# One list schedule for everything up to the branch, and the second phase's buffers laid by the first phase's grounds

## The chip, the core and the metric

The kernel runs on one core of one Trainium2 chip. The metric is the device time of one execution in microseconds (us), lower being better.

## What is computed

One layer of a hybrid decoder over 4096 tokens of width 1024, batch 1, one layer deep:

```python
h = rmsnorm(x, g_pre) * (1 + scale) + shift          # shift, scale, gate = silu(c) @ ada_w + ada_b
proj = h @ w_in                                      # 1024 -> 3328, split by heads
attn = sliding_window_attention(aq, ak, av, sinks) * silu(ag)   # window 128, ALiBi
rkv  = rkv + (shift1(rkv) - rkv) * mu_rkv
rwkv = rwkv7(h, rr, rk, rv, ...) * silu(rg)          # delta rule, a state of 64x64 per head
gla  = gla(h, gq, gkk, gv, ...) * silu(gg)           # gated linear attention in chunks
y = concat([attn, rwkv, gla]) @ w_out
return x + gate * rmsnorm(y, g_post)
```

## The kernel before

The tokens are cut into NS = 16 tiles of NT = 256. Products with the large weights are made of float16 parts: each weight and each activation is split into a high and a low half, and three products of halves are added.

Phase 1 goes over the 16 tiles and does the normalisation, the recurrent groups (RWKV-7 and GLA) and all preparation. Its stages are generators: `stage_a` (norm and transposes of tile i, hT), `stage_p` (projections; it has the values "vg" ready first, then x1, then the k, r and v rows), `stage_d` (decays), `stage_qa`, `stage_qb`, `stage_qc` (matrix AT, its transfer through DRAM as adr into AS, a serial inverse TT in 15 steps on VectorE, its transfer as tdr into td, the assembled inverse tf), `stage_v`, `stage_k` (BK from KB), `stage_r` (GLA), and `stage_q2` (the recurrence over four chunks: rp, up, sp, and the state Sst from Ss and cd; then the normalised output ysb, sent to DRAM as mscr). Beside them run three streams of preparation:

- `stage_l` splits the later phase-1 weights.
- `stage_c(i)` splits the seven weights of phase 2 (w2): for each, eight pieces are loaded (cs) and squared, the sum goes through a matmul, and the pieces are loaded again, split (ch) and stored (wscr). After that it takes the squares of the output weight (`wo_squares`, twice 16 pieces) and forms and splits its combinations (`wo_group`, 16 of them, stored as woscr). `stage_c(i)` waits for `stage_c(i-1)` and for tile i's "vg".
- `stage_g` forms the adaLN gate from ada_w on GpSimd: two halves (gacc) of four blocks, each of two loads (gaw) with products and sums, then one pair of matmuls (gp) and a store.

`emit()` runs the generators by rank (a lower rank first) against an estimated TensorE clock and so writes the program; the place in it is each step's rank. While it is written, `Order.note` records each instruction with its estimated cost and what it must follow: readers and writers of the same data, the turn of a tile in its ring of buffers, the PSUM banks. `Order.pin()` then makes a list schedule of all recorded steps: engine by engine, the step that can start first and, among those, the one of lowest rank. It pins that order with dependencies which cost no semaphore. The rank of evictions in phase 2 is lowered by URGENT = 150.

Phase 1's buffers lie in five pools, work1a to work1d (the tuple `order` says which tag goes into which of the first three, the rest go into d) and c1p. After phase 1 these pools close, and phase 2 opens its own on the same ground: work2k (q, kT, vt, v4), c2p (ab), wg (weights q5 and q6), work2m (mxa, mxb), work2p (pr), work2o (yv, sm1), wb (output weights). The framework adds the waits that this reuse needs.

Then comes what is written ahead of a branch: the load of the weights (`stage_w`), the first projections (`stage_first`: `qkv(0)` with kp, two qp and vp; `gates(0)` with four gp, on q3 to q6; `qkv(1)`), tile 0's attention (`stage_s(0)`: scores sc into pr, exponentials, transposes, products ovp), and the loads of the output weights. The branch itself (line 1967) takes a slow path when a gate is out of limits, which it isn't with these inputs. In the kernel before, `pin()` is called at the end of phase 1, inside its block, and `forget()` throws away what was recorded from there to the branch: those instructions have no list schedule and are ordered by the framework alone. Behind the branch phase 2's main loop is recorded and pinned by a second `pin()`.

All instructions are issued through `Lane`, so the profile gives line 330 for nearly all of them, and names of tiles tell them apart. DMAs go through SP's one queue, in order.

Of the kernel before, what the change touches and what calls it, by code (L numbers as in the profile page):

```python
# [25 lines left out]
NS = T // NT  # L26
# [20 lines left out]
class Pool:  # L47


    def __init__(self, pool, bufs, held):  # L50
        self.pool, self.bufs, self.held = pool, bufs, held

    def tile(self, shape, dt, bufs=None, **kw):
        t = self.pool.tile(shape, dt, **kw) if bufs is None else self.pool.tile(shape, dt, bufs=bufs, **kw)
        self.held[t.tensor.name] = self.bufs if bufs is None else bufs
        return t


# [6 lines left out]
class Order:  # L65
# [2 lines left out]

    def __init__(self, tc):
        self.tc, self.held, self.masks, self.lag, self.urgent, self.joint = tc, {}, {}, 0, 0, 0  # L70
        self.steps = []
        self.wrote, self.read, self.users, self.slots, self.known = {}, {}, {}, {}, set()

    def pool(self, pool, bufs=1):
        return Pool(pool, bufs, self.held)

    def region(self, ap):

# [20 lines left out]
    def note(self, eng, name, outs, ins, func, r):  # L99
# [7 lines left out]
        n = max(math.prod(a.shape[1:]) for a in [o, *ins[:1]])  # L107
# [60 lines left out]
        for t, tensor in tiles.items():  # L168
            if t not in self.known:
                self.known.add(t)  # L170
                if t in self.held and tensor.tag:
                    held = self.slots.setdefault((tensor.owner_uid, tensor.tag), [])

                    if held and self.users.get(held[-1]):
                        st.turn.append(self.users[held[-1]][0])
                    if len(held) == self.held[t]:
                        for j in self.users.get(held.pop(0), ()):
                            need(j)
                    held.append(t)
            elif t in self.held and self.users.get(t):  # L180
                st.turn.append(self.users[t][0])
            if str(tensor.space) == "PSUM":
                for j in self.users.get(t, ()):
                    need(j)
# [209 lines left out]
def hybrid_kernel(ctx, tc, x, vecs, rows, adaw, w1, wl, w2, wo, w2aug, a2, gk2, cst, ctr, ctg, abias, out):  # L394
    nc = tc.nc
    model = Model(tc)
# [6 lines left out]
    def pool_of(at, name, bufs=1, **kw):  # L403
        return model.order.pool(at.enter_context(tc.tile_pool(name=name, bufs=bufs, **kw)), bufs)
# [141 lines left out]
    def streams(*lst):  # L546
        for rank, name, gen, i in lst:
            live.append([rank, i if i is not None else 0, name, gen(i), (), 0.0, ()])
# [92 lines left out]
    with ExitStack() as p1:  # L641
# [2 lines left out]
        pp = pool_of(p1, "c1p", 1)  # L644
        order = (("hf", "gl", "b1", "zs", "gw", "cgc", "bl", "gk1s", "zl0", "zl1", "zl2", "ch", "cl", "cs"),
                 ("zb0", "zb1", "zb2", "ta", "ep", "em", "b2", "KB"),
                 ("qg", "kg", "egp", "egm", "vg", "c2", "kt", "cd", "em0"))

        def wt(shape, name, bufs=1, dt=F32, tag=None):
            tag = tag or name  # L650
# [283 lines left out]
        def stage_c(i):  # L934

            yield [("c", i - 1), ("vg", i)]
            if 6 <= i < 8:
                yield from wo_squares(i - 6)
            elif 8 <= i < NS - 2:
                for g in range(i - 8, 16, 6):  # L940
                    yield from wo_group(g % 4, g // 4)
            for n in range(7):
                if n != i:
                    continue
                src = w2[:, n * 2048 : (n + 1) * 2048]
                inv = w_inv[n]


                def piece(j):
                    s32 = wt([P, 256], "cs", 2)  # L950
                    SP.dma_start(s32, src[:, j * 256 : (j + 1) * 256])
                    return s32

                ss = st.tile([P, 2, KD], F32, tag="wss8", name="wss8")
                for j in range(KD):
                    s32 = piece(j)
                    yield [s32]
                    S.activation(wt([P, 2, 256], "ch", 2, F16)[:, 0], s32, AF.Square, accum_out=ss[:, 0, j : j + 1])
                    if n == 2:
                        S.activation(wt([P, 2, 256], "ch", 2, F16)[:, 0][:, 0:P], s32[:, 0:P], AF.Square, accum_out=ss[:, 1, j : j + 1])  # L960
                yield [ss]
                parts = ((0, inv, None),) if n != 2 else ((0, inv, None), (1, k_sc[:, 1:2], k_sc[:, 0:1]))
                sc = st.tile([P, 1], F32, tag="wsc", name="wsc")
                for o, iv, sx in parts:
                    sst = st.tile([P, 1], F32, tag="wss", name="wss")
                    V.tensor_reduce(sst, ss[:, o, :], axis=AX.X, op=ALU.add)
                    yield [sst, "mq"]
                    sp = mq("wssp")
                    PE.matmul(sp[:, 0:1], ones, sst, start=True, stop=True)
                    tot = st.tile([P, 1], F32, tag="wtot", name="wtot")  # L970
                    V.tensor_copy(tot, sp[:, 0:1])
                    pow2(sc if sx is None else sx, iv, tot)
                for j in range(KD):
                    s32 = piece(j)
                    yield [s32]
                    hi, lo = [t[:, n] for t in (wt([P, 2, 256], "ch", 2, F16),) for n in range(2)]
                    S.activation(hi, s32, AF.Identity, scale=sc)
                    V.scalar_tensor_tensor(lo, s32, sc, hi, op0=ALU.mult, op1=ALU.subtract)
                    SP.dma_start(wscr[n, :, 0, j * 256 : (j + 1) * 256], hi)
                    SP.dma_start(wscr[n, :, 1, j * 256 : (j + 1) * 256], lo)  # L980
                if n == 2:

                    V.tensor_scalar(kq_s, inv, k_sc[:, 0:1], 2.0**-13, op0=ALU.mult, op1=ALU.mult)
                    V.tensor_mul(fneg[:, 0:1], hinv, k_sc[:, 1:2])
                    for m in range(2):
                        f2 = lsc.rearrange("p (v j) -> p v j", v=2)[:, :, 2 * m : 2 * m + 2]
                        V.tensor_scalar(fneg[:, 1:2], fneg[:, 0:1], w_inv[m], 2.0**26 * HD ** -0.5, op0=ALU.mult, op1=ALU.mult)
                        V.tensor_copy(f2, fneg[:, 1:2].rearrange("p (o q) -> p o q", o=1).to_broadcast([P, 2, 2]))
                    V.tensor_single_scalar(fneg, lsc, -1.0, op=ALU.mult)
                    V.reciprocal(fiv, lsc)  # L990
                    V.tensor_mul(sinks, sinks, fiv)
                V.tensor_scalar(inv, inv, hinv, None, op0=ALU.mult)
                if n > 2:
                    V.tensor_single_scalar(g_h[n - 3], inv, 0.5, op=ALU.mult)

        def stage_g(_):

            for g in range(2):
                acc = wt([P, 4, P], "gacc", 1)
                for n in range(4):  # L1000
                    yield [("a", 1 + 4 * g + n)]
                    for h in range(2):
                        aw = wt([P, 4, P], "gaw", 2)
                        SP.dma_start(aw, adaw[8 + 2 * g + n // 2, :, 4 * h : 4 * h + 4, (n % 2) * P : (n % 2 + 1) * P])
                        yield [aw]
                        G.tensor_tensor(aw, aw, scol[:, 4 * h : 4 * h + 4].rearrange("p (k o) -> p k o", o=1).to_broadcast([P, 4, P]),
                                        op=ALU.mult)
                        G.tensor_tensor(aw[:, 0:2, :], aw[:, 0:2, :], aw[:, 2:4, :], op=ALU.add)
                        if h:
                            G.tensor_tensor(aw[:, 0, :], aw[:, 0, :], acc[:, n, :], op=ALU.add)  # L1010
                        G.tensor_tensor(acc[:, n, :], aw[:, 0, :], aw[:, 1, :], op=ALU.add)
                yield [acc, "m"]
                gp2 = mt("gp2")
                PE.matmul(gp2, ones, acc.rearrange("p n c -> p (n c)"), start=True, stop=True)
                gr = acc.rearrange("p n c -> p (n c)")
                V.tensor_copy(gr[0:1, :], gp2[0:1, :])
                SP.dma_start(gscr[:, g * 512 : (g + 1) * 512], gr[0:1, :])
# [544 lines left out]
            SP.dma_start(mscr[i][:, 0 : 2 * NT], mix.rearrange("p b n -> p (b n)"))  # L1562
            E[i] = {n: E[i][n] for n in ("bl", "zl")}

        streams((9, "l", stage_l, None), (11, "g", stage_g, None))
        for i in range(NS):
            streams((0, "q2", stage_q2, i), (1, "k", stage_k, i), (2, "qc", stage_qc, i), (3, "qb", stage_qb, i),
                    (4, "qa", stage_qa, i), (5, "v", stage_v, i), (6, "r", stage_r, i), (7, "w", stage_d, i),
                    (8, "a", stage_a, i), (9, "c", stage_c, i), (10, "p", stage_p, i))
        emit()  # L1570
        model.order.pin()


    def pool2(name):
        return pool_of(ctx, name, 1, reuse_waits="tile")

    w2k, pp, wg, w2m, w2p, w2o, wb = [pool2(n) for n in ("work2k", "c2p", "wg", "work2m", "work2p", "work2o", "wb")]
    pools = {"q": w2k, "kT": w2k, "vt": w2k, "v4": w2k, "mxa": w2m, "mxb": w2m, "pr": w2p, "yv": w2o, "sm1": w2o}

    def wt(shape, name, bufs=1, dt=F32):  # L1580
# [365 lines left out]
    tiles_o = [(Wv, 0), *((Wr[n], n) for n, stays in PRODUCTS if stays)]  # L1946
    for t, n in tiles_o:
        load_o(t, n)


    flag = nc.values_load(fi[0:1, 0:1], min_val=0, max_val=1)
# [157 lines left out]
```

## Time and profile before

| | us |
|---|---|
| median of 3 runs | 2119.78 |
| lowest and highest | 2119.0, 2122.61 |
| the profiled execution | 2119.1 |
| its span, first to last instruction | 2117.3 |

| engine | busy us | share of the span |
|---|---|---|
| PE (matmul) | 1968.9 | 93% |
| PEld (weight loads) | 1544.7 | 73% |
| DVE (VectorE) | 1645.2 | 78% |
| ACT (ScalarE) | 1149.6 | 54% |
| POOL (GpSimd) | 210.1 | 10% |

In rows of a timeline the columns are start and duration in us, engine, line, operation, written tile <- read tiles, shape and count, and in brackets the idle time of the engine before it with what ended that. In a table of windows they are the window, its length, busy time and count for PE, weight loads, DVE, ACT and POOL, the clock granted to PE as a part of full speed, the busy share of the DMA engines, and GB/s. In rows of one tile they are the durations (least, median, most) in ns and the starts of the first and the last in us. In DMA rows the last number is the us from issue to landing. The chain of waits gives start, us and what ran.

### The profile page before, as it was taken

How to read it: one execution, taken by the hardware profiler on the slowest of the kernel's cores; microseconds unless marked ns; L12 is line 12 of the kernel's file. 1: busy time of each engine (PE TensorE's matmuls, PEld its weight loads, DVE VectorE, ACT ScalarE, POOL GpSimd, SP SyncE). 2: the span in 40 equal slices, each digit the busy share in tenths (PEclk: the TensorE clock that was granted, in tenths of full speed). 3: DMA queues.
4: the chain of work that ended last, by engine and by line, in shares of the span. 5: the costliest groups of instructions: out<-in, count | busy, mean ns of one | idle time of the engine just before them, and what ended most of it. 6: DMA issues, size and time to landing. Idle time of an engine off the chain costs nothing. (4 is left out here: it accounts for less than half of the span.)

```text
span 2117.3 us, 61691 instructions
## 1 busy us (share of the span) xinstructions
PE 1968.9 (93%) x24951; PEld 1544.7 (73%) x24951; DVE 1645.2 (78%) x5261; ACT 1149.6 (54%) x2755; POOL 210.1 (10%) x403
## 2 busy tenths in 40 slices
PE   4799999999999999979778999999999999999996
PEld 3577787887878778767557777777777777777773
DVE  7777769887877777887865888777878877778876
ACT  3776677766777667565324444534344444444442
POOL 2311112111111111101310000000000000000000
PEclk8899999999999999989888999999999999999998
DMA  9332132233242122244515343433343333334341
GB/s 293 127 111 80 64 97 81 73 104 105 89 119 84 53 79 77 94 133 130 160 54 186 125 162 103 134 107 118 113 141 123 123 123 112 112 124 143 105 139 73
DMA packets 187192, 241.96 MB, mean 114 GB/s; under 512 B 52163, under 2 KB 145812, under 8 KB 182678
## 3 DMA queue, kind: packets, MB, share of 16 engines
q1 hardware_dynamic: 185220, 236.76, 35.2%
q8 instruction: 197, 3.23, 0.6%
q10 hardware_dynamic: 1682, 1.21, 0.2%
q14 instruction: 93, 0.76, 0.1%
HBM read 177.08 MB, written 60.82 MB: 112 GB/s over the span
## 5 line engine op out<-in xcount | busy, mean ns | idle before, releaser
L330 PEld LDWEIGHTS <-mtp 128*128 128x128 f16 x1344 | 130.4, 98 | 142.3 <-issue 3.5
L330 PE MATMUL op<-o,mtp 128*128 128x512 f16 x768 | 171.9, 380 | 0.0
L330 ACT ACTIVATE pr<-pr,nm,lsc 128x256 f32<-128x256 f32 (+1 forms) x256 | 149.2, 585 | 38.7 <-DVE nm L330 36.7
L330 PE MATMUL op<-ov,mtp 128*128 128x512 f16 x576 | 144.8, 381 | 2.1 <-ACT mtp L330 2.1
L330 PEld LDWEIGHTS <-hT 128*128 128x128 f16 x1536 | 121.8, 101 | 23.7 <-issue 3.8
L330 DVE TENSOR_TENSOR yv<-op,yv 128x512 f32<-128x512 f32 x112 | 75.2, 682 | 56.6 <-PE op L330 41.3
L330 DVE CUSTOM_DVE_ANT_0 pr<-sc,ab,sinks 128x256 f32<-128x256 f32 (+1 forms) x256 | 108.0, 476 | 8.9 <-PE sc L330 7.7
L330 PE MATMUL pv<-gvh,hT 128*128 128x272 f16 x512 | 102.3, 290 | 3.5 <-DVE zb L330 1.8
L330 ACT ACTIVATE mtp<-yv,oi 128x1024 f16<-128x1024 f32 x32 | 36.6, 1144 | 126.7 <-DVE yv L330 125.3
L330 ACT ACTIVATE ag<-gp,gh 128x512 f32<-128x512 f32 x64 | 43.7, 683 | 110.9 <-PE gp L330 110.9
L330 POOL COPY kT<-kT 128x512 f16<-128x512 f16 x15 | 9.7, 646 | 870.8 <-DVE kT L330 870.8
L330 PE MATMUL lp<-hT,Lh 128*128 128x256 f16 x512 | 90.8, 273 | 2.1 <-ACT vg L330 1.1
L330 PE MATMUL zz<-hT,kh 128*128 128x256 f16 x512 | 92.5, 273 | 0.0
L330 PE MATMUL zz<-hT,rh 128*128 128x256 f16 x512 | 91.2, 275 | 0.0
L330 DVE SCALAR_TENSOR_TENSOR ag<-ag,gp 128x512 f32<-128x512 f32 x64 | 43.8, 684 | 60.4 <-ACT ag L330 60.4
L330 PE MATMUL sc<-kT,q 128*128 128x256 f16 (+1 forms) x512 | 72.3, 273 | 19.1 <-DVE m L330 12.7
L330 PE MATMUL qp<-hT,q1h 128*128 128x256 f16 x512 | 87.5, 276 | 1.3 <-DVE kT L330 1.3
L330 PE MATMUL gqk<-hT,gqkh 128*128 128x256 f16 x512 | 87.2, 273 | 1.0 <-DVE zb L330 1.0
L330 PE MATMUL zz<-hT,vh 128*128 128x256 f16 x512 | 87.9, 273 | 0.0
L330 PE MATMUL qp<-hT,q0h 128*128 128x256 f16 x512 | 85.3, 273 | 2.2 <-DVE yv L330 1.5
L330 PE MATMUL gp<-hT,q5h 128*128 128x256 f16 x512 | 87.2, 273 | 0.0
L330 PE MATMUL gp<-hT,q4h 128*128 128x256 f16 x512 | 85.9, 273 | 0.9 <-issue 0.9
(435 smaller groups left out, 6108.7 us busy)
## 6 DMA issues: line engine op xcount, KB each, us to landing
ov<-woscr SPq DMA_DIRECT2D x96, 512.0 KB, 3.7
xt<-in_x SPq DMA_DIRECT2D x16, 1024.0 KB, 5.4
hscr<-hT SPq DMA_DIRECT2D x16, 1024.0 KB, 5.4
hT<-hscr SPq DMA_DIRECT2D x16, 1024.0 KB, 4.8
out<-yv SPq DMA_DIRECT2D x32, 512.0 KB, 2.9
x<-in_x SPq DMA_DIRECT2D x30, 512.0 KB, 4.2
cs<-in_w SPq DMA_DIRECT2D x112, 128.0 KB, 2.5
v<-vscr SPq DMA_DIRECT2D x128, 64.0 KB, 3.2
```

What stands on the lines that cost most here:

```text
L330: r = f(*args, **kw)
```

## The change

1. `pin()` moves from the end of phase 1 to just ahead of the branch, behind `load_o`. So one list schedule covers phase 1, the weight loads, the first projections, tile 0's attention and the output weights' loads.
2. Each pool of phase 2 gets a list `over` of the phase-1 pools on whose ground it lies. When a tile of such a pool is first used, the schedule lets that step follow every recorded user of every tile of those pools. This changes the planned order; the waits on the chip are still the framework's.
3. The pools of phase 2 are opened in another order, so they lie elsewhere: pr behind ab and on work1b, mxa and mxb on work1b and work1c, the weights q5 and q6 on work1c.
4. The tags gacc and gaw go from work1d to work1c.
5. `stage_c`: the seven splits are given to tiles 0 to 4 (1, 2, 1, 2, 1), the output weight's squares to tiles 4 and 5, its 16 groups to tiles 6 to 13, two each. Before, the splits were on tiles 0 to 6, the squares on 6 and 7 (ahead of that tile's split), and the groups on 8 to 13, up to three each.
6. `stage_g` has rank 9 and not 11, and its block n of half g waits for `stage_q2(4g + n)` where it waited for `stage_a(1 + 4g + n)`.

```diff
@@ Order.note
                 self.known.add(t)
+                for old in self.home[t].over if t in self.home else ():
+                    for name in old.names:
+                        for j in self.users.get(name, ()):
+                            need(j)
@@ phase 1's tags
-                 ("qg", "kg", "egp", "egm", "vg", "c2", "kt", "cd", "em0"))
+                 ("qg", "kg", "egp", "egm", "vg", "c2", "kt", "cd", "em0", "gacc", "gaw"))
@@ stage_c
             yield [("c", i - 1), ("vg", i)]
-            if 6 <= i < 8:
-                yield from wo_squares(i - 6)
-            elif 8 <= i < NS - 2:
-                for g in range(i - 8, 16, 6):
-                    yield from wo_group(g % 4, g // 4)
-            for n in range(7):
-                if n != i:
-                    continue
+            for n in ((0,), (1, 2), (3,), (4, 5), (6,))[i] if i < 5 else ():
...
+            if 4 <= i < 6:
+                yield from wo_squares(i - 4)
+            elif 6 <= i < NS - 2:
+                for g in (i - 6, i + 2):
+                    yield from wo_group(g % 4, g // 4)
@@ stage_g
-                    yield [("a", 1 + 4 * g + n)]
+                    yield [("q2", 4 * g + n)]
@@ streams
-        streams((9, "l", stage_l, None), (11, "g", stage_g, None))
+        streams((9, "l", stage_l, None), (9, "g", stage_g, None))
...
-        model.order.pin()
-
-    def pool2(name):
-        return pool_of(ctx, name, 1, reuse_waits="tile")
-
-    w2k, pp, wg, w2m, w2p, w2o, wb = [pool2(n) for n in ("work2k", "c2p", "wg", "work2m", "work2p", "work2o", "wb")]
+        (wka, wkb, wkc, wkd), c1p = wk1, pp
+
+    def pool2(name, *over):
+        t = pool_of(ctx, name, 1, reuse_waits="tile")
+        t.over = over
+        return t
+
+    w2k, pp, w2p, w2m, wg, w2o, wb = [pool2(*n) for n in (
+        ("work2k", wka), ("c2p", wka, wkb), ("work2p", wkb), ("work2m", wkb, wkc), ("wg", wkc), ("work2o", wkc, wkd),
+        ("wb", wkd, c1p))]
@@ ahead of the branch
         load_o(t, n)
+    model.order.pin()
```

More of the change, by code (lines that the diff above doesn't have):

```diff
@@ L47, with __init__ @@
 class Pool:
-    def __init__(self, pool, bufs, held):
-        self.pool, self.bufs, self.held = pool, bufs, held
+    def __init__(self, pool, bufs, held, home):
+        self.pool, self.bufs, self.held, self.home, self.over, self.names = pool, bufs, held, home, (), []
     def tile(self, shape, dt, bufs=None, **kw):
@@ L55, in tile @@
         self.held[t.tensor.name] = self.bufs if bufs is None else bufs
+        self.home[t.tensor.name] = self
+        self.names.append(t.tensor.name)
         return t
@@ L70, in __init__ @@
         self.tc, self.held, self.masks, self.lag, self.urgent, self.joint = tc, {}, {}, 0, 0, 0
-        self.steps = []
+        self.steps, self.home = [], {}
         self.wrote, self.read, self.users, self.slots, self.known = {}, {}, {}, {}, set()
     def pool(self, pool, bufs=1):
-        return Pool(pool, bufs, self.held)
+        return Pool(pool, bufs, self.held, self.home)
     def region(self, ap):
```

## The prediction

> **What bounds the kernel now.** I read the table of windows first, then the timelines of the engines around the change of phases, then the DMA issues and the chain of waits. The windows cut the execution where its character changes; the columns are the window, its length, busy time and count on PE, weight loads, DVE, ACT and POOL, the granted PE clock, the DMA share and GB/s.
>
> ```profile
> span 2117.3 us, 61691 instructions
> 0.00:1012.00 1012.00, 930.01 (x13854) 761.12 (x13855) 798.42 (x2881) 675.91 (x1556) 172.94 (x348) 0.97 0.35 106
> 1012.00:1060.00 48.00, 33.89 (x620) 25.02 (x618) 37.82 (x100) 16.92 (x43) 21.98 (x31) 0.85 0.49 138
> 1060.00:1080.00 20.00, 11.73 (x60) 7.81 (x60) 16.42 (x62) 5.20 (x10) 4.49 (x7) 0.58 0.08 19
> 1080.00:1147.00 67.00, 59.98 (x890) 48.51 (x888) 37.62 (x140) 24.89 (x73) 2.18 (x5) 0.96 0.42 130
> 1147.00:1160.00 13.00, 9.76 (x92) 9.15 (x93) 6.30 (x22) 2.02 (x6) 0.00 (x0) 0.68 0.63 215
> 1160.00:2117.00 957.00, 923.56 (x9442) 693.14 (x9439) 748.63 (x2061) 424.70 (x1070) 8.47 (x13) 0.99 0.37 121
> ```
>
> Before 1012 and after 1160 the matmuls are nearly back to back. Between them lie 148 us in which PE is busy for 115.4 and idle for 32.6; its clock falls to 0.58. Counting busy time times (1 - clock), the slow clock costs another 15.5. Since PE is the bound after 1160, the change is worth what it takes out of these 48.1 us, which is a ceiling, less what it costs earlier. What PE waits for there:
>
> ```profile
> 1036.55 0.34 PE L330 MATMUL up<-rs,tf 64*64 64x64 f32 x1 [4.42 <-DVE tf L330]
> 1057.76 0.95 ACT L330 ACTIVATE kT<-kp,kq_s 64x256 f16<-64x256 f32 x2
> 1067.04 0.47 DVE L330 SCALAR_TENSOR_TENSOR kT<-kp,kq_s,kT 64x256 f16<-64x256 f32 x1
> 1071.38 0.59 PE L330 MATMUL qp<-hT,q1h 128*128 128x256 f16 x2 [1.28 <-DVE kT L330]
> 1104.54 0.29 DVE L330 TENSOR_TENSOR Sst<-Ss,cd 128x128 f32<-128x128 f32 x1
> 1114.04 0.69 DVE L330 TENSOR_TENSOR ysb<-ysb,bon 128x512 f32<-128x512 f32 x1 [2.41 <-ACT ysb L330]
> 1114.65 0.34 DVE L330 CUSTOM_DVE_ANT_0 pr<-sc,ab,sinks 128x128 f32<-128x128 f32 x1
> 1150.24 0.80 PE L330 MATMUL sc<-kT,q 128*128 128x256 f16 x3 [3.29 <-PEq L1967]
> 1151.04 4.74 PE vp L330 x48
> ```
>
> Phase 1 ends in a serial chain: tile 14's recurrence, tile 15's triangular inverse, and tile 15's recurrence, whose last state product is at 1104.54. Call that end E. Beside it the first projections of phase 2 are meant to fill PE. They stop when both "pj" banks hold results whose eviction (kT) has not come, and the next one, q1, begins only at 1071.38. After E, tile 0's attention runs: its first score eviction waits at 1114.65 behind tile 15's ysb, and from there 32 us pass to the branch, which stops PE for 3.29. The 48 vp matmuls of tile 1 come behind the branch, in 4.74 at a low clock.
>
> **The change part by part.** *The gate's blocks.* Stage g's second half runs now in the tail:
>
> ```profile
> 1018.00:1064.00 46.00, 16.70 (x24) 0.80 0.44 124
> 1032.96 1.01 DVE L330 TENSOR_TENSOR cs<-cs 128x128 f32<-128x128 f32 x1
> 1048.91 0.28 DVE L330 TENSOR_TENSOR cs<-cs 128x128 f32<-128x128 f32 x1
> 1090.40 0.86 DVE L330 COPY tf<-X 32x256 f32<-32x256 f32 x2 [0.88 <-PE X L330]
> 1045.76 1.94 SPq L330 DMA_DIRECT2D gaw<-in_adaw  x2
> 1049.55 0.47 SPq L330 DMA_DIRECT2D AS<-adr  x1
> 1064.69 1.92 PE L330 MATMUL gp<-gacc,ones 128*128 128x512 f32 x2
> ```
>
> The first row is POOL's work on the blocks: 16.70 us in 46. While a block is on POOL, a DVE product of two SBUF tiles takes 1.01; without one the same product takes 0.28. The slow ones stand ahead of tile 14's copy into tf, for which PE waited 4.42; tile 15's copy waited for PE alone, 0.88. So 3.5 us of tile 14's chain go, and the two gaw issues, 1.94, go from SP's queue ahead of tile 15's AS loads. I take 5 of the 5.4, since the output weights' blocks stay in DVE's queue. With the new rank and the waits on q2 both halves are emitted among the first nine tiles, and the sums' two matmul pairs move into full PE time: 1.92 at a clock near 0.58 is 1.1, twice, so +2. Beside POOL DVE loses at most 16.7 x (1 - 0.28/1.01) = 12 us there. DVE is idle for 213 of the first 1012, which hides it: I take 0 and keep 12 for the range. Below nothing isn't in reach, since these blocks add work to that part. The Trainium skill speaks against the move here: "GPSIMD Engine Reference", section 1 "Specifications", has the SBUF interfaces of GpSimd shared with VectorE, with contention for two-input instructions. The 1.01 against 0.28 agrees.
>
> *The weights' splits.* The diff puts seven splits into five tiles and the output weights' sums from tile 4 on.
>
> ```profile
> L330 ACT ACTIVATE ch<-cs,wsc x56: 491/507/511, 141.0 to 764.5; 128x256 f16<-128x256 f32 x56
> L330 ACT ACTIVATE ch<-cs,wo_sc x64: 386/495/527, 861.0 to 1051.2; 128x256 f16<-128x256 f32 x48, 128x128 f16<-128x128 f32 x16
> 532.31 0.51 ACT L330 ACTIVATE ch<-cs,wsc 128x256 f16<-128x256 f32 x1
> 534.17 0.42 ACT L330 ACTIVATE ch<-cs 128x256 f16<-128x256 f32 x1
> 1054.19 0.68 DVE L330 SCALAR_TENSOR_TENSOR ch<-cs,wo_sc,ch 128x256 f16<-128x256 f32 x1
> ```
>
> The seventh split ends at 764.5, though its gate is the values of tile 6, and sixteen tiles in 1012 us put that near 440. One split's last piece (532.31) is followed by the next one's first square (534.17). So stage c is a chain of its own, which runs behind its gates, and loosening gates that do not hold moves nothing. The sixteen groups of the output weights still start near 861 and end near 1055. I take 0 and keep a gain for the rivals.
>
> *The grounds.* work2k lies on work1a, where ch and cs are. The list now holds q and kT back until every reader of work1a is done, so the eviction of kT stays near 1057, as in the trace. Behind it DVE's half waited to 1067.04 among tile 15's inverse and tile 14's norm, and their rank stays ahead of kT. A few us of idle go at 1060 to 1080, but the work they admit is done early only if the chain, not PE, is late. I take 2, from 0 to 4. pr moves from ground shared with late tiles to work1b, whose last reader (KB) is done before E. The scores still need the "sq" bank, which E frees. So the first pr comes some 2 us after E and not 10.
>
> The weights q5 and q6, however, move onto work1c, and there cd is read by the product at 1104.54. Now they are issued at 1081:
>
> ```profile
> 1081.11 0.34 SPq L330 DMA_DIRECT2D q5h<-wscr  x1
> q5h<-wscr SPq DMA_DIRECT2D x1, 512.0 KB, 3.7
> 1245.68 11.90 PE gp L330 x109
> 1266.26 2.62 PE kp L330 x24
> 1268.88 5.25 PE qp L330 x48
> ```
>
> In the changed kernel they cannot come before E, and land 3.7 later at the soonest. The two gate products on them and tile 1's kp and qp follow in the order of the "pj" banks: 96 x 11.90/109 = 10.5, 2.62 and 2 x 5.25 = 10.5, then vp, 4.74 x 0.68 = 3.2; 26.8 us of PE, beside tile 0's attention.
>
> *The one list.* From E to the end of tile 1's vp, at 1151.04 + 4.74 = 1155.78, pass 51.2 us. In the windows 1080 to 1160 PE is idle for 7.0 + 3.2 and loses 2.4 + 3.1 to its clock, 15.7 together. The branch's 3.29 and the 3.1 behind it stay; 9.3 can go. Of this I give back 2 for the new wait on q5, the rest of its 3.7 being covered by scores: 7. Both ends of it agree: with E at 1099.5, tile 0's attention (32 us from a first pr 2 us after E) ends at 1133.5, and PE, with 3.7 + 26.8 us and the scores to fit in, some us behind that, where the branch now comes at 1147.
>
> The sum: -5 (blocks) +2 (their matmuls) -2 (kT) -7 (from E to the branch) = -12. The profiled execution took 2119.1 us (its span 2117.3), so 2107.1; the median of the runs is 0.7 above it, so 2107.8. The work after the branch is the same, and the main loop's buffers only lie elsewhere: 0, with 3 either way for a list that starts from another moment.
>
> **The rivals.** *The splits do come forward.* If the c chain was held by its gates in the emission, the groups end before tile 15 and DVE's load in 1012 to 1060 (37.82 of 48) goes. Then kT is evicted near 1030 and that window's idle 14.1 and 5.1 of slow clock go too: -12 - 19 = -31, 2088.8. The row at 534.17 speaks against it.
>
> *The blocks cost what the tail gains.* If the 12 us of DVE come up on PE in the full part, because PE's small products wait for DVE there directly, +12 meets -12: 2119.8. For it speaks that DVE is busy for 79% of that time; against it, that those stretches are filled by projections of another tile. This is the page's contention taken at its full size.
>
> *SP's queue stops.* The list places fourteen weight loads in SP's one queue, among the last tiles' adr, AS, tdr and td transfers, each at the time at which its costs put the release of a slot or ground. Where PE is later than that, the load stands at the head, and the transfers behind it wait, on the chain to E. Each us there moves E one for one. It decides from 12 us on; two stops of 10, one on each of the last two tiles' chains, give +8: 2127.8. For it: AS already stood behind gaw in that queue, and PE waited 4.42 at a point where a filler could have run. Against it: the loads up to q1 are ready early in the trace.
>
> **How the numbers follow.** A measurement of this kernel can tell about 0.2%, 4.2 us, from no change. The forecast has 0.48; alone it runs from -20 (E earlier by all 5.4, the whole 9.3, kT's 4, a start 3 better, +2) to -6 (nothing for kT, the 3.7 given back whole, a start 3 worse), 2100 to 2114. The splits coming forward have 0.14, the blocks' cost 0.13 and SP's stops 0.25. Faster is 0.48 + 0.14 = 0.62, same 0.13, slower 0.25. The range from 2086 to 2128 leaves out about half of the second case and under half of the last, 0.18.
>
> **What would show it.** Right: gaw on POOL ends by the middle of phase 1; PE waits for tf of tile 14 for about 1 us; ch still ends near 1050; the first pr follows tile 15's last Sst by 2 to 4 us; q5h is issued after that Sst; the branch's stop comes near 1137. Wrong: ch ending before 1000 (the first rival); PE busy under 925 in the first 1012 us (the second); an SP issue of a q load that lasts several us with td or AS behind it, and E after 1105 (the third).

## The result, and the profile after

| | median us | runs |
|---|---|---|
| before | 2119.33 | 12 (2114.54 to 2123.57) |
| changed | 2121.03 | 12 (2117.77 to 2126.41) |

The ratio is 1.0009, 95% interval 0.9999 to 1.0020: no difference that this measurement can tell. The forecast was -12 us.

The profiled execution of the changed kernel was the slowest of its twelve (2126.4) and reaches the end of tile 13 6.5 us later than the kernel before; a_v below, whose stages up to there are the same, reaches it at 998.0, as the kernel before does. So I compare stretches between events and not absolute times. Its table of windows, cut as in the prediction:

```profile
span 2124.6 us, 61681 instructions
0.00:1012.00 1012.00, 932.08 (x13845) 758.02 (x13846) 805.22 (x2882) 673.75 (x1562) 195.48 (x372) 0.98 0.36 110
1012.00:1060.00 48.00, 43.90 (x753) 35.60 (x753) 34.05 (x100) 18.40 (x41) 8.45 (x13) 1.00 0.21 63
1060.00:1080.00 20.00, 5.79 (x44) 3.84 (x42) 13.56 (x74) 7.28 (x15) 0.00 (x0) 0.62 0.20 53
1080.00:1147.00 67.00, 51.96 (x704) 43.77 (x704) 29.70 (x124) 20.77 (x62) 2.18 (x5) 0.73 0.37 119
1147.00:1160.00 13.00, 6.17 (x107) 5.23 (x108) 6.75 (x16) 1.92 (x6) 0.00 (x0) 0.50 0.17 47
1160.00:2117.00 957.00, 930.62 (x9504) 698.55 (x9502) 748.12 (x2064) 425.04 (x1071) 8.46 (x13) 1.00 0.37 123
```

The hole moved. 1012 to 1060 is full now (43.90 busy at clock 1.00, from 33.89 at 0.85), but 1060 to 1147 is emptier: 57.75 busy where there were 71.71. The rows that carry this, in time order (timelines, two rows of tiles, and the DMA view):

```profile
L336 POOL TENSOR_TENSOR gaw<-gaw,scol x16: 1039/1062/2017, 27.5 to 436.0; 128x512 f32<-128x512 f32 x16
L336 ACT ACTIVATE ch<-cs,wo_sc x64: 385/497/513, 807.9 to 996.9; 128x256 f16<-128x256 f32 x48, 128x128 f16<-128x128 f32 x16
1004.80 0.29 DVE L336 TENSOR_TENSOR Sst<-Ss,cd 128x128 f32<-128x128 f32 x1
1020.16 0.95 ACT L336 ACTIVATE kT<-kp,kq_s 64x256 f16<-64x256 f32 x2
1060.06 0.29 DVE L336 TENSOR_TENSOR Sst<-Ss,cd 128x128 f32<-128x128 f32 x1
1077.21 0.37 SPq L336 DMA_DIRECT2D q5h<-wscr  x1
1102.91 0.29 DVE L336 TENSOR_TENSOR Sst<-Ss,cd 128x128 f32<-128x128 f32 x1
1103.23 0.32 SPq L336 DMA_DIRECT2D q6h<-wscr  x1
1108.03 0.63 PE L336 MATMUL gp<-hT,q5h 128*128 128x256 f16 x2
1118.99 3.73 SPq L336 DMA_DIRECT2D o<-woscr  x6
1122.76 11.29 SPq L336 DMA_DIRECT2D v<-vscr  x8
1135.64 1.09 PE L336 MATMUL ovp<-pr,v 32*64 32x128 f32 x40
1136.76 0.48 DVE L336 CUSTOM_DVE_ANT_0 pr<-sc,ab,sinks 128x256 f32<-128x256 f32 x1 [1.74 <-PE ovp L336]
1156.91 0.59 PE L336 MATMUL gp<-hT,q3h 128*128 128x256 f16 x2 [3.85 <-PEq L1976]
o<-woscr SPq DMA_DIRECT2D x8, 512.0 KB, 9.9
```

The first two rows are the blocks' products on GpSimd, the last of them at 436.0 where it was at 1060.4, and the output weights' groups, which start at 807.9 and not at 861.0. The three Sst rows are the last state products of tiles 13, 14 and 15 (the last is E). The row at 1136.76 is a score eviction of tile 0's second half, which waited for the first half's ovp. The row with PEq is the first instruction behind the branch. Of the kernel before, two rows of the same timeline and one of SP's are needed beside those of the prediction:

```profile
998.28 0.28 DVE L330 TENSOR_TENSOR Sst<-Ss,cd 128x128 f32<-128x128 f32 x1
1057.47 0.28 DVE L330 TENSOR_TENSOR Sst<-Ss,cd 128x128 f32<-128x128 f32 x1
1119.71 5.99 SPq L330 DMA_DIRECT2D v<-vscr  x8
```

From such rows come the stretches of every kernel. The column "to 13" is not read from a trace, since single executions reach that point up to 12 us apart in kernels whose stages up to there are the same (992.9 in a_cd, 1004.8 in the changed kernel). It is the ratio times 2117.0 (about the median of the kernel before), less 1.8 outside the span, less the other four stretches, which come from one trace of each kernel, and is good to some 3 us.

| kernel | ratio (95%) | to 13 | 13 to 14 | 14 to E | E to branch | behind it |
|---|---|---|---|---|---|---|
| before | 1 | 996 | 59.2 | 47.1 | 45.7 | 967.1 |
| changed | 1.0009 (0.9999, 1.0020) | 997 | 55.3 | 42.9 | 54.0 | 967.7 |
| a_v | 0.9973 (0.9962, 0.9983) | 996 | 55.5 | 42.8 | 47.5 | 967.8 |
| a_cd | 1.0036 (1.0021, 1.0050) | 998 | 55.2 | 49.5 | 52.0 | 968.2 |
| a_cdv | 0.9976 (0.9966, 0.9987) | 996 | 55.2 | 49.5 | 42.0 | 967.9 |
| a_hold | 0.9969 (0.9957, 0.9981) | 996 | 55.2 | 44.0 | 46.0 | 967.9 |
| a_listonly | 1.0025 (1.0015, 1.0036) | 994 | 61.5 | 45.9 | 52.5 | 967.1 |
| b_c | 0.9978 (0.9965, 0.9991) | 994 | 56.3 | 46.7 | 46.3 | 967.1 |
| b_g | 0.9982 (0.9970, 0.9994) | 996 | 53.8 | 47.2 | 46.5 | 967.5 |
| b_cg | 1.0001 (0.9990, 1.0011) | 1000 | 54.2 | 46.3 | 47.4 | 967.6 |
| a_vpj | 0.9968 (0.9954, 0.9983) | 995 | 61.0 | 40.6 | 43.8 | 968.0 |
| a_vg | 0.9973 (0.9964, 0.9983) | 999 | 55.5 | 42.8 | 47.2 | 964.9 |
| a_best | 0.9962 (0.9950, 0.9975) | 999 | 55.3 | 45.3 | 40.7 | 966.7 |
| a_best_c | 0.9942 (0.9929, 0.9954) | 990 | 62.4 | 43.7 | 41.1 | 965.9 |
| a_sp | 1.0006 (0.9993, 1.0019) | 997 | 57.5 | 41.3 | 53.1 | 967.4 |
| a_sp2 | 1.0031 (1.0019, 1.0043) | 1003 | 57.7 | 41.2 | 52.6 | 967.3 |
| a_best_sp | 0.9932 (0.9909, 0.9955) | 994 | 58.0 | 43.2 | 40.6 | 964.9 |
| a_best_sp2 | 0.9964 (0.9951, 0.9978) | 1000 | 57.5 | 42.9 | 41.4 | 966.3 |

The change took 3.9 us out of tile 14 and 4.2 out of tile 15, and lost 8.3 between E and the branch and 0.6 behind it. So E does come 8 us earlier after tile 13, and all of it is given back.

### The profile page after: what moved, and what is told of

Same layout as the page of the kernel before. It is cut to its first block, busy times and chain, and to the rows that moved or that the text cites. A ratio compares the mean times of both kernels' runs of the same rounds, so it can differ in the third digit from the quotient of the medians.

```text
span 2124.6 us, 61681 instructions
## 1 busy us (share of the span) xinstructions
PE 1970.5 (93%) x24951; PEld 1545.0 (73%) x24951; DVE 1640.6 (77%) x5261; ACT 1147.2 (54%) x2755; POOL 214.6 (10%) x403
## 5 line engine op out<-in xcount | busy, mean ns | idle before, releaser
L336 DVE TENSOR_TENSOR yv<-op,yv 128x512 f32<-128x512 f32 x112 | 75.1, 681 | 56.6 <-PE op L336 41.4
L336 ACT ACTIVATE ag<-gp,gh 128x512 f32<-128x512 f32 x64 | 43.6, 683 | 107.2 <-PE gp L336 107.2
L336 DVE SCALAR_TENSOR_TENSOR ag<-ag,gp 128x512 f32<-128x512 f32 x64 | 43.8, 684 | 64.0 <-ACT ag L336 63.9
L336 PE MATMUL gp<-hT,q3h 128*128 128x256 f16 x512 | 85.4, 273 | 4.2 <-PEq L1976 3.8
L336 PE MATMUL sc<-kT,q 128*128 128x256 f16 (+1 forms) x512 | 72.4, 275 | 15.7 <-DVE m L336 15.7
```

The source lines that it names most:

```text
L336: r = f(*args, **kw)
```

## The experiments

Three theories on where it went. **T1**: the fill. q5 and q6 now lie where cd is read until E, so their products start at 1108, PE runs empty and slow from 1060 on, and that delays what follows. **T2**: the values' trip. Tile 0's v goes through DRAM; its loads now stand in SP's queue behind six output-weight loads (o) of 512 KB, so ovp comes late. **T3**: what the tail gained is lost in the full part of phase 1, where the blocks and splits now lie. Kernels named a_ start from the changed one, those named b_ from the one before.

**The values ahead of the output weights (a_v).** Each step of the output weights' loads must follow tile 0's last load of v:

```diff
     SP.dma_start(v4[a][32 * g : 32 * g + 32], ...)
+        f["vstep"] = len(model.order.steps) - 1
...
     for t, n in tiles_o:
         load_o(t, n)
+    for step in model.order.steps[first_o:]:
+        step.needs[F[0]["vstep"]] = False
```

> The changed kernel, but the loads of the output weights' pieces (o) may stand in the list only after tile 0's loads of v, as they stood in the kernel before. T2: the product ovp of tile 0's first half starts near 1126 instead of 1135.6 and the branch and the time come 9 us earlier. T1: PE is still starved and slow in 1060 to 1108; the branch comes earlier by what the values' trip alone held, 5 to 9 us. T3: within 4 us of the changed kernel.

Timeline rows of this kernel:

```profile
1096.31 0.29 DVE L336 TENSOR_TENSOR Sst<-Ss,cd 128x128 f32<-128x128 f32 x1
1113.45 4.32 SPq L336 DMA_DIRECT2D v<-vscr  x8
1118.82 5.04 SPq L336 DMA_DIRECT2D o<-woscr  x8
1119.10 1.09 PE L336 MATMUL ovp<-pr,v 32*64 32x128 f32 x40
1143.78 0.58 PE L336 MATMUL gp<-hT,q3h 128*128 128x256 f16 x2 [3.90 <-PEq L1980]
```

The eight issues of v take 4.32 us in place of 11.29, ovp starts 22.8 after E and not 32.7, the branch 6.5 earlier after E, and the ratio falls by 0.0036, 7.6 us. Nothing else moved in the table by more than 1 us. T2 holds: 6.5 to 7.6 us where 9 was expected.

**The fill before E (a_cd, a_cdv).** cd and em0 leave the ground of q5 and q6; a_cdv has the edit of a_v as well:

```diff
-   ("qg", "kg", "egp", "egm", "vg", "c2", "kt", "cd", "em0", "gacc", "gaw"))
+   ("qg", "kg", "egp", "egm", "vg", "c2", "kt", "gacc", "gaw"))
```

> The changed kernel, but cd and em0 no longer lie in work1c, the ground that q5 and q6 are laid on; they keep their places in the part of the ground that phase 2's first weights do not use. T1 (the fill ends because q5 and q6 wait for the last reader of cd): q5h is issued before 1060 and not at 1077, the gate products on q5h run before the last state product instead of from 1107.8 on, PE's clock stays above 0.5 in 1070 to 1110, the chunks of the last recurrence take 3.3 us and not 3.95, and the time falls by 5 (only E earlier) to 25 us (all of PE's idle and slow clock there). T2 (tile 0's values come late behind the output weights' loads): PE's fill moves but the branch stays within 3 us of E + 50, and the time falls by 5 at most. T3 (the loss lies in phase 1's full part): within 4 us of the changed kernel.

> Both edits: cd and em0 out of work1c, and the loads of o behind those of v. T1 and T2 together: E near 1100, the branch near 1137 (from 1155), the time 15 to 20 us under the changed kernel, some 2102. If only one of them holds, this gives what that one gives alone. T3: within 4 us of the changed kernel, and what was gained earlier is not visible in the branch's time.

Rows of a_cd, from timelines of PE and DVE:

```profile
1048.09 0.29 DVE L336 TENSOR_TENSOR Sst<-Ss,cd 128x128 f32<-128x128 f32 x1
1055.97 0.58 PE L336 MATMUL gp<-hT,q5h 128*128 128x256 f16 x2 [1.47 <-DVE ag L336]
1084.28 0.29 DVE L336 TENSOR_TENSOR Sst<-Ss,cd 128x128 f32<-128x128 f32 x1
1089.62 0.29 DVE L336 TENSOR_TENSOR Sst<-Ss,cd 128x128 f32<-128x128 f32 x1
1097.62 0.29 DVE L336 TENSOR_TENSOR Sst<-Ss,cd 128x128 f32<-128x128 f32 x1
1128.62 1.97 PE L336 MATMUL ovp<-pr,v 32*64 32x128 f32 x40 [11.70 <-DMA v<-vscr]
```

The fill came forward as meant (1055.97 for 1108.03), and PE's hole before E closed. The time rose by 0.27%, 5.7 us. Tile 14's end to E is 49.5 where it was 42.9. Of these 6.7 us, 5.2 lie ahead of tile 15's first state product, where its inverse is put together (1048.09 to 1084.28 is 36.2; in the changed kernel it was 31.0), and 1.5 in the recurrence, whose second chunk takes 5.34 (1084.28 to 1089.62). The list fixes the order on each engine, and the pieces of tile 1's projections and their evictions now stand between the links of the chain. Behind E, PE then waits 11.70 for v. With the loads of v in order (a_cdv) E to the branch falls to 42.0, but what that wins over a_v (5.5) is no more than what E lost (6.7), and the two ratios can't be told apart: some 7 us under the changed kernel, not the 15 to 20 of both together. T1 is wrong: closing PE's hole before E won nothing.

**Only tile 1's projections held (a_hold).** a_cdv, with tile 1's first kp bound in the list to the last state product (a cut of the edit; `estep` is that step, and the list lets the first use of a tile in `behind` follow the step named there):

```diff
+    if i == 1:
+        model.order.behind[kp.tensor.name] = [model.estep]
```

> The kernel with cd and em0 out of work1c and the loads of o behind those of v, and the first projection of tile 1 made to wait for the last state product. Theory: it is the fill laid between the links of the last chain (tile 1's kp and qp from 1075 on) that lengthened tile 14's end to the last state product from 42.8 to 49.5; q5 and q6 alone lie where DVE works on the triangular inverse and cost 1 us. Then that stretch is 43 to 45 and the stretch to the branch stays near 42: 3 to 5 us under the kernel without the wait, some 2107. Rival: the early weight loads on the DMA queues are what delays the chain, or q5's and q6's products do; then it stays at 48 to 50, and with tile 1's projections behind the last state product the time is 0 to 4 us longer.

Tile 14's end to E is 44.0 again: of the 6.7 us, 5.6 were tile 1's kp and qp between the links, and 1.1 are left for q5, q6 and their loads. The stretch to the branch went to 46.0, not the 42 that I expected, so the projections cost nearly as much behind E (4.0) as before it. The ratio is 0.0007 under a_cdv's, which is not distinguishable.

**The spreads, apart from the list (a_listonly, b_c, b_g, b_cg).** a_listonly has stages c and g as before; b_c, b_g and b_cg put the new stage c, the new stage g, or both into the kernel before.

> The changed kernel with stages c and g as they were before: the seven splits in seven tiles, the output weights' sums from tile 6 on, the gate's second half by its old waits and rank 11. The list and the grounds stay as changed. If the spread of splits and blocks is what moved stage c from 861 to 808 (so that its gates do hold), the output weights' groups start near 861 again and end near 1054, kT is evicted near 1057, tile 14's copy into tf waits 4 us for DVE, and the time is above the changed kernel by 5 to 15 us. My prediction's reading (stage c is a chain of its own that no gate holds): the groups start at 808 here too, and only the blocks' 3 to 5 us come back. T3 (the spread costs in the full part what the tail gains): phase 1's projections are 10 us earlier and the time is no worse than the changed kernel's.

> The kernel before, with stage c alone as changed: seven splits in five tiles, the output weights' sums from tile 4 on. If the gates in the emission hold stage c (against my prediction), the output weights' groups start near 808 here and end near 998, kT is evicted near 1030, tile 14 ends 3 to 5 us sooner after tile 13, and the time is 3 to 8 us under the kernel before. If stage c is a chain of its own, the groups start near 861 as before and the time is that of the kernel before.

> The kernel before, with stage g alone as changed (rank 9, the second half's blocks wait for the values and not for the attention). The gate's blocks leave the last tiles: tile 14's copy into tf waits about 1 us and tile 14 ends 3 to 5 us sooner after tile 13. If the blocks on GpSimd also held stage c (DVE's products of the sums take 1.01 us beside them and 0.28 without), the groups start before 861; if not, they stay there. Time: 2 to 5 us under the kernel before. If the blocks' work between 400 and 440 us costs what the tail gains (the rival of the prediction), the time is that of the kernel before.

> The kernel before with both spreads, without the one list and its grounds. If spread and list are two separate effects of opposite sign, this one has tile 14's end 4 us and the last state product 8 us sooner after tile 13 than the kernel before, keeps its 45.7 us from there to the branch (the values go ahead of the output weights there), and is 4 to 8 us faster than the kernel before. If the spread alone brings nothing and the list only gives back what its own order costs, it is within 3 us of the kernel before. If the spread costs in the full part (T3), it is slower.

Rows of tile ch and of ACT's timeline in b_c, then of tile ch in b_g:

```profile
L330 ACT ACTIVATE ch<-cs,wo_sc x64: 385/507/537, 796.7 to 991.6; 128x256 f16<-128x256 f32 x48, 128x128 f16<-128x128 f32 x16
1021.29 0.93 ACT L330 ACTIVATE kT<-kp,kq_s 64x256 f16<-64x256 f32 x2
```

```profile
L330 ACT ACTIVATE ch<-cs,wo_sc x64: 385/506/532, 798.9 to 973.1; 128x256 f16<-128x256 f32 x48, 128x128 f16<-128x128 f32 x16
```

Either edit alone starts the output weights' groups near 798 and not 861; in a_listonly they start at 856.7, and kT is evicted at 1056. So stage c is held by what the program's writing does, and the step that said it was not is wrong. Why stage g's rank alone also moves it wasn't tried. In all three b_ kernels kT comes at 1012 to 1021, and yet 14 to E and E to the branch stay within 1.7 us of the kernel before: kT's late eviction had cost little there. What each edit wins alone, 4 to 5 us, lies in tile 14 (2.9 and 5.4) and, as far as its 3 us of doubt let one say, for b_c ahead of it. Both together win nothing: tile 14 keeps its 5.0, and the part up to tile 13 is 4 longer. That is T3's loss, beside T2's. For the list and the grounds without the spreads, a_listonly gives +0.25%; E to the branch (+6.8) is T2's again, with v's loads behind six of o. That is some 3 us above the changed kernel, where 5 to 15 were expected.

**vp earlier (a_vpj, a_vg).** a_v, with tile 0's vp on the pj banks: directly behind q in a_vpj, between the second and the third gate product in a_vg.

```diff
-        yield ["mq"]
-        vp = mq("vp")
+        yield ["mq"] if i else ["pj"]
+        vp = mq("vp") if i else pjt("vp")
```

> The changed kernel with the loads of o behind those of v, and tile 0's product vp put on the pj banks behind q (where nothing of phase 1 goes) instead of on the bank that tile 15's transposed output uses. T2 carried on: the values' trip through DRAM is over before the last state product; the first ovp follows the transposes of pr, some 16 us after the last state product instead of 23, and the time is 5 to 8 us under that of the kernel with the loads alone in order, some 2104. If something else is late next (the second half's scores on their banks, the output weights' loads), it is 0 to 3 us. If vp's 4.8 us ahead of the gate's products delay the serial chain as the earlier fill did, it is slower by up to 5.

> The changed kernel with the loads of o behind those of v, and tile 0's product vp put between the second and the third gate product, on the pj banks: there PE has run out of work in the trace of the changed kernel (from 1049). If what was lost with vp ahead of the gates was only that it lay in front of tile 14's chain, tile 14 ends 55 to 56 us after tile 13 again (there 61.0), the last state product comes 43 to 44 us later, the branch 43 to 44 after that (47.5 with the loads alone in order): 2.5 to 4 us under that kernel, some 2107. If any PE work before the last state product costs the chain what it saves behind it, the time is within 1.5 us of that kernel.

In a_vpj v is loaded from 1029.73 on, E to the branch is 43.8 (3.7 less), but tile 14 takes 61.0 (5.5 more) and tile 15 40.6: the ratio is a_v's within the interval. In a_vg tile 14 is at 55.5 again, the branch did not come earlier, and 2.9 us lie behind it, since tile 1's vp now runs ahead of the branch; a_v's ratio once more. The expectation that ovp would start 16 us after E was met in part (18.3 in a_vpj).

**All of it (a_best, a_best_c).** a_hold with a_vg's place for vp; a_best_c has stage g as before the change on top of that.

> All of it: loads of o behind v, cd and em0 out of work1c, tile 0's vp between the gate products, tile 1's projections behind the last state product. If the two effects are separate, stretch by stretch: 55.5 to tile 14's end, 44 to the last state product, 40 to 42 to the branch, 968 after it, some 2105, 0.5 to 0.65% under the kernel before. If the branch is bound by the second half of tile 0's attention whatever stands ahead of it, 2107 to 2109.

> The same with stage g as in the kernel before (rank 11, the blocks behind the attention) and only the splits spread. In the kernel before each spread alone saved 4 us and both together nothing, since the part up to tile 13 then took 4 us more. If that cost of the two together is real, the part up to tile 13 is 2 to 4 us shorter here; against it the blocks are on GpSimd in the last tiles again, so tile 14 comes 1 to 2 us later: 0 to 3 us under the kernel with both. If it was chance of the runs, the time is 1 to 3 us above it.

Rows of DVE's and PE's timeline in a_best_c:

```profile
988.59 0.28 DVE L338 TENSOR_TENSOR Sst<-Ss,cd 128x128 f32<-128x128 f32 x1
1050.99 0.28 DVE L338 TENSOR_TENSOR Sst<-Ss,cd 128x128 f32<-128x128 f32 x1
1094.73 0.29 DVE L338 TENSOR_TENSOR Sst<-Ss,cd 128x128 f32<-128x128 f32 x1
1135.79 0.59 PE L338 MATMUL gp<-hT,q3h 128*128 128x256 f16 x2 [3.79 <-PEq L1992]
```

Together the edits (a_best) give 40.7 from E to the branch, 13 under the changed kernel, but the ratio is 0.9962 and not the 0.5 to 0.65% less that I expected: "to 13" is 999. With the blocks left late (a_best_c) the time is 12.3 us under the kernel before (0.9942), though tile 14 then takes 62.4: it reaches the end of tile 13 some 9 us sooner than a_best. This version beats both kernels, by 0.6%.

**Blocks apart (a_sp, a_best_sp, a_sp2, a_best_sp2).** In 400 to 460 us, where the changed kernel has the second half's four blocks at once, its table of windows has PE less busy than the kernel before; first the changed kernel, then the one before:

```profile
400.00:460.00 60.00, 55.38 (x835) 43.99 (x822) 47.05 (x161) 36.73 (x92) 26.08 (x39) 0.94 0.41 122
```

```profile
400.00:460.00 60.00, 60.00 (x973) 49.54 (x972) 51.77 (x187) 45.30 (x95) 12.36 (x22) 1.00 0.25 76
```

In a_sp (on the changed kernel) and a_best_sp (on a_best) the blocks wait for the values of tiles 6, 8, 10 and 12; in a_sp2 and a_best_sp2 each is also bound in the list to the step before it.

```diff
-   yield [("q2", 4 * g + n)]
+   yield [("q2", (n, 6 + 2 * n)[g])]
...
+   if g:
+       model.order.behind[aw.tensor.name] = [len(model.order.steps) - 1]
```

> The changed kernel with stage g's second half let in one block per two tiles (behind the values of tiles 6, 8, 10 and 12) in place of all four at once. If it is the bunch on GpSimd at 400 to 440 us that costs (PE busy 55.4 of 60 at a clock of 0.94 there, 60.0 at 1.00 in the kernel before), the blocks cost less apart: the part up to tile 13 is 4 to 8 us shorter, tile 14 still follows 55 us later, and the time is 4 to 8 us under the changed kernel. If the blocks cost the same wherever they lie in the full part (DVE's products at 1.01 us beside them), the time is within 2 us of the changed kernel. If that stretch is slow for another reason (the splits), there is no difference either, and PE's busy time in 400 to 460 stays at 55.

> The kernel with all four edits (loads of o behind v, cd and em0 out of work1c, vp between the gate products, tile 1's projections behind the last state product), and the blocks one per two tiles. It should keep that kernel's 55 to tile 14's end, 45 to the last state product and 41 to the branch, and, if the bunch is what costs, have the part up to tile 13 of the kernel with the blocks left late (989 against 998): 2099 to 2104. If not: 2107 to 2110.

> As the kernel that lets the blocks in one per two tiles, but now each block of the second half is bound in the list to a step of its tile: there the list had still run all four by 433 us, since nothing but the emission held them and GpSimd was free. If the bunch costs: PE busy 60 of 60 at 400 to 460 as in the kernel before, the part up to tile 13 is 4 to 8 us shorter than in the changed kernel, tile 14 follows 55 us later, time 2111 to 2115. If the blocks cost the same wherever they lie: within 2 us of the changed kernel.

> The same on the kernel with the four mendings. If the bunch costs: 55 to tile 14's end, 45 to the last state product, 41 to the branch, 967 behind it, and the part up to tile 13 at 990 to 994: 2099 to 2104 as a median. If not: 2103 to 2109, as with the blocks all at once.

a_sp told nothing of the bunch: the list still ran the blocks by 434 us, since a wait in the writing holds back no step that has no need of its own, and its time is the changed kernel's. a_best_sp reached 2102.9, but its six runs go from 2093.9 to 2108.8, so whether it is better than a_best isn't settled. In a_sp2 the blocks lie between 578 and 945 us. The last is in the window 900 to 980, where PE is busy for less than in the changed kernel; the rows are a_sp2, the changed kernel and a_sp:

```profile
900.00:980.00 80.00, 66.57 (x1143) 52.27 (x1142) 65.12 (x216) 50.27 (x109) 16.93 (x30) 0.96 0.40 119
```

```profile
900.00:980.00 80.00, 76.17 (x1218) 61.80 (x1215) 64.14 (x220) 51.38 (x114) 11.31 (x25) 0.96 0.45 134
```

```profile
900.00:980.00 80.00, 70.06 (x1108) 54.24 (x1109) 65.14 (x223) 49.52 (x113) 14.31 (x28) 0.94 0.38 113
```

This loss can't be put down to the block: a_sp, which has none there, is at 70.06, and the kernel before, whose later blocks come behind 1010, is at 66.84. a_sp2 is 4.7 us slower than the changed kernel, and a_best_sp2 equals a_best. So laying the blocks apart won nothing, and nothing here bears out that the bunch is what costs.

Three pairs differ in stage g alone; "to 13" grows by 0 (before to b_g), 6 (b_c to b_cg) and 9 (a_best_c to a_best), each good to some 3 us. The window 400 to 460 shows the same loss in all three: PE is busy for 55.8, 56.0 and 54.9 with the blocks there, and for 59.9 to 60.0 without. b_g first, then b_c:

```profile
400.00:460.00 60.00, 55.80 (x810) 44.33 (x809) 45.15 (x160) 37.60 (x95) 25.49 (x40) 0.94 0.41 121
```

```profile
400.00:460.00 60.00, 59.87 (x970) 49.31 (x969) 50.96 (x188) 45.50 (x94) 11.94 (x22) 1.00 0.25 76
```

In b_g the output weights' groups came forward too (798.9), as they do in b_c without that loss. So a reading that fits is that either edit brings stage c forward, which can be won only once, and that the second one adds nothing but the blocks' cost. No run separates this, and which engine carries the cost is open.

## Why the prediction was wrong, step by step

**The failing step is the one from E to the branch.** It took PE's idle time and slow clock there (15.7) as what can go, took off the branch's own part, and counted -7. Measured: +8.3. PE was not what ended that stretch: tile 0's vp, its eviction, the trip of v through DRAM, ovp and the second half follow one another (the eviction at 1136.76 waited for ovp), and the new list put six 512 KB loads ahead of v. a_v shows 6.5 of the 8.3 by that order alone. The prediction listed the output weights' loads as part of the list and never asked what they would be queued ahead of. Where the remaining 1.8 over the kernel before come from was not isolated: q5's and q6's products and tile 1's kp and qp run behind E in both kernels (from 1104.57 before, from 1108.03 now). Ahead of E the terms came to -5 (-5 +2 -2) and some -7 was measured (+1 -3.9 -4.2), partly by luck, as the paragraphs on the blocks and on kT say.

**The rival on SP's queue** had the queue and, by chance, the size (+8), but another place and another stop: it looked for a weight load that waits for its ground at the head of the queue, ahead of td and AS before E. There E came early; what cost time was the order behind E.

**The ceiling of 48.1 us** was the wrong frame. Filling PE's hole before E made the kernel slower (a_cd), and in b_c the window 1012 to 1060 became nearly full (43.6 busy at clock 1.00) while tile 14's end to E fell by 0.4 only.

**The blocks, -5 +2**: right that the tail gains, near the size. 3.9 us went from tile 14 (5.4 in b_g), but stage c left the tail as well in both, so the blocks' own share is not separated there; the pairs that have stage c forward on both sides give 2.1 (b_c to b_cg) and 7.1 (a_best_c to a_best). The copy into tf no longer follows DVE products of 1.01 (timeline of the changed kernel):

```profile
1039.20 0.85 DVE L336 COPY tf<-X 32x256 f32<-32x256 f32 x2 [0.15 <-PE X L336]
```

The zero for what the move costs in the full part was wrong: the rival "blocks cost what the tail gains" had that, 0 to 9 us by the pairs above against its 12; the +2 for the matmuls can't be told apart in that. The Trainium skill's "GPSIMD Engine Reference", section 1 "Specifications", names contention between GpSimd and VectorE on their SBUF interfaces; that PE loses 4 to 5 us at 400 to 460, where GpSimd does the blocks, agrees with it, but no run here separates that contention from the blocks' loads.

**The splits, 0**: wrong in the step (one split's last piece directly followed by the next one's square does not show that no gate holds the chain as a whole), right that there was little in it: b_c's kT came 36 us sooner and E to the branch stayed. The first rival was right that the groups come forward (they end at 996.9 in the changed kernel), but its -19 for that was wrong as well.

**kT, -2**: kT came at 1020.16 and not near 1057, and 14 to E fell by 4.2, for another reason than the one given. No gate product or projection stands on PE in the last 26 us before E in the changed kernel, so the chain had PE to itself, at the lower clock. In the kernel before and in the three b_ kernels, which have kT early and 46 to 47 us, the traces have 67 to 97 gate matmuls there.

**q5 and q6 behind E, +2 given back**: only q6 was held until E (issued at 1103.23). q5 went out at 1077.21, 26 us before E, against the prediction, and its product ran at 1108.03 all the same, since the list has it there; it waited for no load. Undoing this cost 6.7 before E, most of it by the projections that came forward with it. The first pr behind the "sq" bank 2 us after E also came true (1105.13), and brought nothing, as ovp waited for v.

## What to carry to other kernels

Idle time of the busiest engine beside a serial chain need not be a reserve: filler laid between the links lengthened the chain here (42.9 to 49.5 us), so measure from event to event along the chain. When a schedule takes in more work, look at every queue for the one small transfer on the path that now stands behind large ones. And a gain from moving work off the tail has to be netted against where the work goes, since two moves that won 4 us each won nothing together here.

## What was not expected of the hardware

PE's granted clock stayed at 0.50 for 40 us in the changed kernel although PE was busy for up to 85% of that time (windows of 10 us):

```profile
1070.00:1080.00 10.00, 3.32 (x12) 2.15 (x12) 3.56 (x12) 4.44 (x10) 0.00 (x0) 0.50 0.33 80
1080.00:1090.00 10.00, 7.35 (x210) 5.86 (x211) 4.75 (x18) 0.52 (x2) 1.57 (x4) 0.50 0.18 68
1090.00:1100.00 10.00, 8.46 (x136) 7.16 (x134) 2.33 (x8) 1.04 (x4) 0.00 (x0) 0.50 0.01 2
1100.00:1110.00 10.00, 6.10 (x48) 4.43 (x46) 6.64 (x44) 3.69 (x14) 0.00 (x0) 0.50 0.32 105
```

A chunk of the recurrence then takes 3.95 us, against 3.30 at clock 1.00 in the kernel before, and the stretch to E was shorter all the same. The Trainium skill's "TensorE: Matmul & The Clock Gate", part 1, gives some 3.4 us of sustained activity for the full clock; this trace shows that a busy share of 0.85 in the profile, made of small matmuls with waits between them, is not that.

SP's queue kept its order under load: eight 64 KB loads of v took 11.29 us to issue behind six of the 512 KB loads, 4.32 ahead of them. The transfers of o themselves took 9.9 from issue to landing in that stretch.
